# The first stage of a recurrent-mixer layer: the norm's sums from rows of tokens, gates in one bank, two whole tiles in the loop

## The chip, the cores and the metric

The kernel runs on one core of one Trainium2 chip. The metric is the device time of one execution in microseconds (us), the median of several runs; lower is better. A change of about 0.2% is the least that can be told from none.

## The reference, cut to what matters

One layer of a decoder trunk: an RMS norm, one wide input projection, four groups of mixers (mLSTM, Mamba-2 SSD, a gated short convolution, RG-LRU), an output projection with a residual, and a last RMS norm, for 1024 prompt tokens and 8 x 4 sample tokens, 1056 in all, with 2048 channels. The change touches the first lines only:

```python
def rms_norm(x, w):
    x32 = x.astype(jnp.float32)
    y = x32 * lax.rsqrt(jnp.mean(x32 * x32, axis=-1, keepdims=True) + EPS)
    return (y * w.astype(jnp.float32)).astype(x.dtype)
...
xn = rms_norm(x, norm_w)
proj = xn @ w_in
(ml_q, ml_k, ml_v, ml_o, ml_z, ml_i, ml_f, ssd_z, ssd_xbc, ssd_dt,
 sc_b, sc_c, sc_h, sc_z, rg_x, rg_z) = split_columns(proj)
```

ml_o and ml_z are split into 128-column tiles, of which o 0 and z 0 are the first two that the kernel computes; the 16 columns of ml_i, ml_f and ssd_dt are the gates.

## The kernel before, in words

Everything lies with channels on the partitions. The input x arrives as 16 tiles k of 128 channels x 1056 tokens (528.5 KB each with the column of the norm's weights). For fp32 accuracy each operand of a matrix product is cut into a high and a low part: `xsplit` makes xh (ScalarE, L469) and xl = x w - xh (VectorE, L472) of a tile, `w_split` makes wh (ScalarE, L260) and wl (VectorE, L261) of a weight piece of two k by 128 columns (128 KB), and `mm6` multiplies with three products for each k: wh xh (L279), wh xl (L280), wl xh (L281). The norm's factor rstd is not needed for the products: it multiplies their results.

`startup` is the first stage. Its loop goes over ke = 0..7, two k at a time, and computes output tile o 0 whole (three PSUM banks of 352 tokens) and two of the three chunks of z 0 (the chunks are 352 tokens wide): 30 products of 128 x 352 in each pass. PSUM has eight banks: five hold these chunks, three hold the gates (`bg`), whose products (L521, plain fp32, 16 columns of weights) come every second pass, four k for each of three chunks, each k to a partition group of its own. Beside the products, `xsquare` gathers the squares for the norm: the square on ScalarE for even k (L478, L483) and on VectorE for odd k (L481), the sum over k on GpSimd (L484), the last two on VectorE. After the loop the third chunk of z 0 is computed by itself with the weights of tile z 0 loaded and cut a second time (48 products), and only then the ordinary loop over tiles begins (`in_proj`, tile 2 of 56). Beside that third chunk the generator `norm_gates` runs: sums over the partitions by TensorE (L338), the root, rstd on all partitions, then the gates' rows.

What sets the order: each engine runs its own instructions in program order. Work of the mixers is written as generators in two lanes; `tick()`, called after each group of six products in `in_proj`, lets each lane go one step. The queue SP issues loads in program order: a load whose buffer isn't free yet holds up all that stand behind it. The input's tiles have 8 buffers (NS, `stage`); the weights' pieces have 3 raw buffers, 5 more in the first stage, and 4 pairs of cut ones (`whl`): `w_next()` cuts the pieces two ahead of the one in use, and so waits for TensorE to release a pair. `in_proj` takes the four banks of `pj()` in turn, and its tile 2 begins with the bank that held the first chunk of o 0, so it waits until that chunk has been copied out (L538).

## Time and profile before

| | |
|---|---|
| device time, median of 3 runs (lowest, highest) | 1838.86 us (1837.83, 1840.14) |
| profiled execution, first to last instruction (its span) | 1837.4 us |
| TensorE busy / ScalarE / VectorE / GpSimd | 1796.7 / 522.8 / 956.9 / 220.1 us |
| first product of the first stage to the first of tile 2 | 5.04 to 87.48 us |

The profile is of one execution; its time is its span, and no other time of that execution is given. The span leaves out what lies before the first and behind the last instruction; the median of the runs is 1.5 us longer. An engine's busy time is summed over the whole span, so a stage in which it waits must be looked at by itself.

### The profile page before, as it was taken

To read this page: it belongs to the slowest core of one execution; us is meant where nothing else is said; L and a number is where in the kernel's file an instruction comes from. 1 tells how busy PE (TensorE), PEld (TensorE's weight loads), DVE (VectorE), ACT (ScalarE), POOL (GpSimd) and SP (SyncE) were. 2 spreads that over 40 slices of the span, in tenths; PEclk is the share of its full clock that TensorE was granted. 3 is DMA by queue.
4 is the path that set the end of the run, shared out by engine and by line. 5 is a ranking of instruction groups with operands and counts; after the bars stand their busy time and mean duration, and the time that the engine had idled before them with its cause. 6 is when DMAs were issued, how large, how long until landed. Compare 5 with 4: busy or idle time off the path is not lost.

```text
span 1837.4 us, 30141 instructions
## 1 busy us (share of the span) xinstructions
PE 1796.7 (98%) x11443; PEld 1762.0 (96%) x11443; DVE 956.9 (52%) x2026; ACT 522.8 (28%) x1244; POOL 220.1 (12%) x248
## 2 busy tenths in 40 slices
PE   7899999999999999999999999999999999999997
PEld 6799999999999999999999999899999999999997
DVE  8875445434624534655357646643773643333664
ACT  4422222212212211221144213211441432222553
POOL 4200101001002000320000003100000221110121
PEclk8999999999999999999999999999999999999998
DMA  6211222212222111331211124321111643332674
GB/s 209 85 47 50 70 58 76 63 60 73 54 70 71 58 59 47 107 77 56 88 43 61 55 69 100 71 82 56 59 58 47 220 125 93 93 93 89 208 251 142
DMA packets 141230, 160.57 MB, mean 87 GB/s; under 512 B 18917, under 2 KB 127997, under 8 KB 140573
## 3 DMA queue, kind: packets, MB, share of 16 engines
q1 hardware_dynamic: 135644, 138.34, 25.4%
q0 software_dynamic: 4704, 18.84, 2.6%
q8 instruction: 89, 1.46, 0.3%
q10 hardware_dynamic: 736, 1.48, 0.3%
q14 instruction: 57, 0.46, 0.1%
HBM read 136.75 MB, written 21.84 MB: 86 GB/s over the span
## 4 chain that ended last, share of the span: by engine, by line
PE 83%; DMA 4%; DVE 3%; issue 1%; ACT 1%; POOL 1%; SPq 0%; DVEq 0%; POOLq 0%; ACTq 0%
PE bank L279 27%; PE bank L281 26%; PE bank L280 26%; DMA arena<-rowd 2%; DVE wl L261 1%; DMA wr<-in_w_in 1%; POOL arena L1073 1%; DVE arena L1082 0%; PE bank L897 0%; PE bank L875 0%; PE bank L896 0%; ACT wh L260 0%; PE bank L899 0%; ACT arena L1060 0%; DMA wr<-in_w_out 0%
## 5 line engine op out<-in xcount | busy, mean ns | idle before, releaser
L279 PE MATMUL bank<-xh,wh 128*128 128x352 f32 x3328 | 1088.3, 327 | 3.2 <-ACT xh L469 2.2
L280 PE MATMUL bank<-xl,wh 128*128 128x352 f32 x3328 | 1076.6, 323 | 13.6 <-DVE xl L472 13.6
L281 PE MATMUL bank<-xh,wl 128*128 128x352 f32 x3328 | 1075.6, 323 | 5.9 <-DVE wl L261 5.7
L280 PEld LDWEIGHTS bank<-xl,wh 128*128 128x128 f32 x3328 | 628.6, 189 | 18.3 <-DVE xl L472 17.9
L279 PEld LDWEIGHTS bank<-xh,wh 128*128 128x128 f32 x3328 | 628.3, 189 | 14.1 <-issue 6.8
L281 PEld LDWEIGHTS bank<-xh,wl 128*128 128x128 f32 x3328 | 628.9, 189 | 7.6 <-DVE wl L261 7.6
L261 DVE TENSOR_TENSOR wl<-wr,wh 128x256 fp32r<-128x256 f32 x540 | 246.1, 466 | 402.7 <-ACT wh L260 401.8
L260 ACT ACTIVATE wh<-wr 128x256 fp32r<-128x256 f32 x540 | 215.6, 412 | 583.7 <-PE bank L280 482.1
L590 DVE TENSOR_TENSOR arena<-bank,arena 128x352 f32<-128x352 f32 x114 | 58.7, 523 | 80.8 <-PE bank L281 80.5
L261 DVE TENSOR_TENSOR wl<-arena,wh 128x256 fp32r<-128x256 f32 x108 | 63.9, 611 | 63.8 <-ACT wh L260 63.3
L1359 POOL TENSOR_TENSOR arena<-arena 128x352 f32<-128x352 f32 x39 | 37.0, 950 | 245.0 <-ACT arena L1358 244.6
L260 ACT ACTIVATE wh<-arena 128x256 fp32r<-128x256 f32 x108 | 42.4, 411 | 78.4 <-PE bank L280 75.0
L941 DVE SCALAR_TENSOR_TENSOR arena<-arena 128x1080 f32<-128x1080 f32 (+1 forms) x44 | 59.9, 1361 | 1.0
L1351 DVE TENSOR_TENSOR arena<-bank,arena 128x352 f32<-128x352 f32 x47 | 24.7, 525 | 41.8 <-PE bank L281 20.1
L1358 ACT ACTIVATE arena<-arena 128x352 f32<-128x352 f32 x44 | 22.0, 500 | 79.9 <-DVE arena L1351 79.9
L279 PE MATMUL bank<-xh,xl 128*128 128x352 f32 x128 | 41.5, 324 | 0.0
L281 PE MATMUL bank<-xh,xl 128*128 128x352 f32 x128 | 41.4, 324 | 0.0
L280 PE MATMUL bank<-xl 128*128 128x352 f32 x128 | 41.1, 321 | 0.0
L929 POOL COPY arena<-arena 128x3 f32<-128x3 f32 (+1 forms) x16 | 3.0, 186 | 296.1 <-DVE arena L585 296.1
L583 DVE TENSOR_TENSOR arena<-bank,arena 128x352 f32<-128x352 f32 x32 | 16.4, 522 | 41.5 <-PE bank L281 41.5
L484 POOL TENSOR_TENSOR arena<-arena 128x1056 f32<-128x1056 f32 x13 | 32.6, 2510 | 35.6 <-DVE arena L481 35.1
L405 DVE RECIPROCAL arena<-arena 128x352 f32<-128x352 f32 (+3 forms) x18 | 35.7, 1981 | 0.2
(332 smaller groups left out, 1288.1 us busy)
## 6 DMA issues: line engine op xcount, KB each, us to landing
wr<-in_w_in SPq DMA_DIRECT2D x441, 128.0 KB, 2.4
wr<-in_w_out SPq DMA_DIRECT2D x130, 128.0 KB, 2.7
arena<-in_w_out SPq DMA_DIRECT2D x126, 128.0 KB, 2.6
arena<-rowd SPq DMA_DIRECT2D x32, 256.0 KB, 5.1
arena<-in_x SPq DMA_DIRECT2D x15, 528.5 KB, 6.3
mixd<-arena POOLq DMA_DIRECT2D x15, 528.0 KB, 3.9
arena<-mixd SPq DMA_DIRECT2D x15, 528.0 KB, 5.9
arena<-in_x SPq DMA_DIRECT2D x16, 352.0 KB, 3.4
```

Source lines behind the costliest of these rows:

```text
L260: self.S.activation(h, r, AF.Copy)
L261: self.V.tensor_sub(l, r, h.bitcast(F32))
L279: self.P.matmul(bank[:, :n], wh[:, k, :], xh, start=first and k == 0, stop=False)
L280: self.P.matmul(bank[:, :n], wh[:, k, :], xl, start=False, stop=False)
L281: self.P.matmul(bank[:, :n], wl[:, k, :], xh, start=False, stop=last and k == 1)
L405: self.V.reciprocal(x[:, a:b], x[:, a:b])
L484: (V if k > 13 else G).tensor_add(acc[:, :NT], acc[:, :NT], sq[k % 2][:, :NT])
L590: V.tensor_mul(a[:, t0:t0 + CH], bank[:, :CH], rs[:, t0:t0 + CH])
L941: V.scalar_tensor_tensor(y[:, :n], a[:, i:i + n], w(i), y[:, :n], op0=OP.mult, op1=OP.add)
L1351: V.tensor_add(y[:, ts], b[:, :w], y[:, ts])
L1358: S.activation(t, y[:, ts], AF.Square)
L1359: (G if nacc[gr] < KT - 1 else V).tensor_add(a[:, ts], a[:, ts], t)
```

## The change

- x is loaded a second time, from a copy in DRAM with tokens as rows (`xr`, 1056 x 2048), in 18 pieces of 128 tokens x 1024 channels (512 KB; the last two have 32 tokens). For each, `rsum` is one ScalarE instruction: the square with its sum along the row into a column of `sums`. `xsquare`, its buffers, GpSimd's adds, VectorE's squares and the sum over partitions by TensorE are gone; `col_rsqrt` adds two columns of `sums` instead.
- The gates lie in one bank: for each k four products of 264 tokens, each token quarter to a partition group of its own, directly behind the products of that pass. Two banks become free.
- z 0 is computed whole in the loop (36 products in each pass); the third chunk's loop and the second load of its weights are gone.
- x has 6 buffers instead of 8, the rows 5. x tile k+6 is loaded behind the gates of k, and row piece k behind that. x tile 1 comes in thirds. `xsplit` of a pass stands one pass ahead.
- The 14 loads of constants move from SP's queue, pass 3, to GpSimd's queue, pass 1.
- `norm_gates` starts with tile 2 instead of with the third chunk.

```diff
-        for n in range(1, len(TILES)):
+        for n in range(2, len(TILES)):
...
-            if self.wi < 18 or not any(r is a for a in self.spare):
+            if self.wi < 10 or not any(r is a for a in self.spare):
...
-    def col_rsqrt(self, acc, w, mul, add, dst, drop=False):
...
+    def col_rsqrt(self, sums, w, mul, add, dst):
...
-        bk = self.mx()
-        for c in range(nb):
-            n = min(128, w - 128 * c)
-            P.matmul(bk[:n, c:c + 1], acc[:, 128 * c:128 * c + n], self.ones, start=True, stop=True)
-        if drop:
-            acc.drop()
-        yield 2
-        V.tensor_scalar(v[:, :nb - 1], bk[:, :nb - 1], mul, add, op0=OP.mult, op1=OP.add)
...
-        V.tensor_scalar(v[:m, nb - 1:], bk[:m, nb - 1:nb], mul, add, op0=OP.mult, op1=OP.add)
+        V.tensor_add(v, sums[:, :nb], sums[:, nb:2 * nb])
+        sums.drop()
+        V.tensor_scalar(v, v, mul, add, op0=OP.mult, op1=OP.add)
...
-            Q.dma_start(a[:src.shape[0], :src.shape[1]], src)
+            self.G.dma_start(a[:src.shape[0], :src.shape[1]], src)
...
-        NS = 8
+        NS, NX, GW = 6, 5, NT // 4
         stage = [self.slot() for _ in range(NS - 1)] + [self.rstd]
-        sq = [self.slot() for _ in range(2)]
-        acc = self.slot()
+        rows = [self.slot() for _ in range(NX)]
...
+        nb = (NT + 127) // 128
+        sums = self.take(2 * nb)
+        V.memset(sums.ap, 1.0)
...
-        Q.dma_start(stage[0][:, 0:CH + 1], self.io["x"][:, 0, 0:CH + 1])
-        self.w_load(1)
-        for c in (1, 2):
-            e = slice(CH * c + 1, CH * c + CH + 1)
-            Q.dma_start(stage[0][:, e], self.io["x"][:, 0, e])
-        self.w_load(2)
-        xload(1)
-        self.w_load(3)
-        xload(2)
-        Q.dma_start(wg.ap, self.io["w_g"].rearrange("p k c -> p (k c)"))
-        self.w_load(4)
-        for k in range(3, NS):
-            xload(k)
-            self.w_load(k + 2)
...
+        def xload(k, parts=1, other=None):
+            n = NT // parts
+            for c in range(parts):
+                e = slice(n * c + (c > 0), n * c + n + 1)
+                Q.dma_start(stage[k % NS][:, e], self.io["x"][:, k, e])
+                if c == 0 and other:
+                    other()
+        def rload(i):
+            if i < 2 * nb:
+                b, h = i // 2, i % 2
+                n = min(128, NT - 128 * b)
+                Q.dma_start(rows[i % NX][:n, :D // 2], self.io["xr"][128 * b:128 * b + n, D // 2 * h:D // 2 * h + D // 2])
+        def rsum(i):
+            if i < 2 * nb:
+                b, h = i // 2, i % 2
+                n = min(128, NT - 128 * b)
+                r = rows[i % NX][:n, :D // 2]
+                S.activation(r, r, AF.Square, accum_out=sums[:n, nb * h + b:nb * h + b + 1])
...
-        def xsquare(k):
-            x = stage[k % NS][:, 1:NT + 1]
-            if k == 0:
-                S.activation(acc[:, :NT], x, AF.Square)
-            else:
-                if k % 2:
-                    V.tensor_mul(sq[k % 2][:, :NT], x, x)
-                else:
-                    S.activation(sq[k % 2][:, :NT], x, AF.Square)
-                (V if k > 13 else G).tensor_add(acc[:, :NT], acc[:, :NT], sq[k % 2][:, :NT])
+        xload(0, 3, lambda: self.w_load(1))
+        self.w_load(2)
+        xload(1, 3)
+        Q.dma_start(wg.ap, self.io["w_g"].rearrange("p k c -> p (k c)"))
+        self.w_load(3)
+        for k in range(2, NS):
+            xload(k)
+            self.w_load(k + 2)
...
-        bz = [self.pj(), self.bank[7]]
-        bg = self.bank[4:7]
+        bz = [self.pj(), self.bank[7], self.bank[6]]
+        bg = self.bank[4]
+        def gates(k):
+            for c in range(4):
+                P.matmul(bg[32 * c:32 * c + 16, :GW], wg3[:, k, 0:16], stage[k % NS][:, GW * c + 1:GW * c + GW + 1],
+                         start=k == 0, stop=k == KT - 1)
+            if k + NS < KT:
+                xload(k + NS)
...
                 self.w_split(2)
-                xsplit(1)
-            else:
-                xsplit(2 * ke)
-                xsplit(2 * ke + 1)
-            for k in (2 * ke, 2 * ke + 1):
...
-            if ke == 0:
+                xsplit(1, 3)
                 V.tensor_mul(wg3[:, :, 0:16], wg3[:, :, 0:16], wg3[:, :, 16:17].to_broadcast([128, KT, 16]))
-            if ke == 3:
-                self.const_loads()
-            if ke:
-                for banks in (bo, bz):
-                    wh, wl = self.w_next()
-                    for c, b in enumerate(banks):
-                        self.mm6(b, wh, wl, ke, CH * c, CH, False, ke == 7)
-            else:
                 w2 = [self.w_next(), self.w_next(0)]
+                xsplit(2)
                 for k in range(2):
                     for banks, w in zip((bo, bz), w2):
                         for c, b in enumerate(banks):
                             self.mm6(b, *w, 0, CH * c, CH, True, False, (k,))
-            if ke % 2:
-                for c in range(3):
-                    for k in range(2 * ke - 2, 2 * ke + 2):
-                        j = 32 * (k % 4)
-                        P.matmul(bg[c][j:j + 16, :CH], wg3[:, k, 0:16], stage[k % NS][:, CH * c + 1:CH * c + CH + 1],
-                                 start=ke == 1, stop=ke == 7)
-                for k in range(2 * ke - 2, 2 * ke + 2):
-                    if k + NS < KT:
-                        xload(k + NS)
-        for a in (*sq, *stage[:-1], wg):
+                xsplit(3)
+            else:
+                for i, banks in enumerate((bo, bz)):
+                    if 2 * ke + 2 + i < KT:
+                        xsplit(2 * ke + 2 + i)
+                    wh, wl = self.w_next()
+                    for c, b in enumerate(banks):
+                        self.mm6(b, wh, wl, ke, CH * c, CH, False, ke == 7)
+            if ke == 1:
+                self.const_loads()
+            for i in {2: (0, 1, 2), 3: (3, 4), 4: (5, 6), 5: (7, 8), 6: (9, 10), 7: (11, 12, 13)}.get(ke, ()):
+                rsum(i)
+            for k in (2 * ke, 2 * ke + 1):
+                gates(k)
+                rload(k)
+        rload(16)
+        rload(17)
+        for i in range(14, 2 * nb):
+            rsum(i)
+        for a in (*stage[:-1], wg):
...
-        o, z, g = self.slot(), self.slot(), self.slot()
-        for c in (1, 0):
+        o, z, g = self.slot(), self.slot(), self.take(GW)
+        for c in range(3):
+            S.activation(o[:, CH * c:CH * c + CH], bo[c][:, :CH], AF.Copy)
             V.tensor_copy(z[:, CH * c:CH * c + CH], bz[c][:, :CH])
-        for c in range(3):
-            S.activation(g[:, CH * c:CH * c + CH], bg[c][:, :CH], AF.Copy)
-        self.lanes[0].append(self.norm_gates(acc, g, o, z))
-        for ke in range(8):
-            wh, wl = self.w_next()
-            self.mm6(self.bank[7], wh, wl, ke, 2 * CH, CH, ke == 0, ke == 7)
-            if ke < 3:
-                S.activation(o[:, CH * ke:CH * ke + CH], bo[ke][:, :CH], AF.Copy)
-            self.tick()
-        S.activation(z[:, 2 * CH:NT], self.bank[7][:, :CH], AF.Copy)
+        S.activation(g.ap, bg[:, :GW], AF.Copy)
+        for a in rows:
+            a.drop()
...
+        self.lanes[0].append(self.norm_gates(sums, g, o, z))
...
-        yield 2
-        yield from self.col_rsqrt(acc, NT, 1.0 / D, EPS, self.rstd[:, :NT], True)
+        yield 3
...
-        for c in range(3):
+        n = NT // 4
+        for c in range(4):
             b = self.mx()
-            ts = slice(CH * c, CH * c + CH)
-            P.matmul(b[:72, :CH], self.selg.ap, g[:, ts], start=True, stop=True)
+            ts = slice(n * c, n * c + n)
+            P.matmul(b[:72, :n], self.selg[32 * c:32 * c + 16, :], g[32 * c:32 * c + 16, :], start=True, stop=True)
             yield 1
-            V.tensor_mul(gt[:72, ts], b[:72, :CH], self.rstd[:72, ts])
+            V.tensor_mul(gt[:72, ts], b[:72, :n], self.rstd[:72, ts])
```

(Comments and empty lines are left out; the host adds `a["xr"] = c(x[:, 1:].T)`.)

ScalarE at the end of the loop and behind it; wh is a cut weight piece, arena the working memory, bank_81 to bank_83 are o 0's chunks, bank_85 holds gates. Before:

```order
L469 ACTIVATE xh<-arena 128x1056 x2
L483 ACTIVATE arena<-arena 128x1056
L260 ACTIVATE wh_74<-arena 128x256
L260 ACTIVATE wh_76<-arena 128x256
L469 ACTIVATE xh<-arena 128x1056 x2
L483 ACTIVATE arena<-arena 128x1056
L260 ACTIVATE wh_70<-wr_67 128x256
L260 ACTIVATE wh_72<-wr_68 128x256
L532 ACTIVATE arena<-bank_85 128x352
L532 ACTIVATE arena<-bank_86 128x352
L532 ACTIVATE arena<-bank_87 128x352
L260 ACTIVATE wh_74<-wr_69 128x256
```

The same place now:

```order
L468 ACTIVATE xh<-arena 128x1056
L260 ACTIVATE wh_76<-arena 128x256
L461 ACTIVATE arena<-arena 128x1024 x2
L260 ACTIVATE wh_70<-wr_67 128x256
L260 ACTIVATE wh_72<-wr_68 128x256
L461 ACTIVATE arena<-arena 128x1024 x5
L461 ACTIVATE arena<-arena 32x1024 x2
L533 ACTIVATE arena<-bank_81 128x352
L533 ACTIVATE arena<-bank_82 128x352
L533 ACTIVATE arena<-bank_83 128x352
L535 ACTIVATE arena<-bank_85 128x264
L260 ACTIVATE wh_74<-wr_69 128x256
```

Seven row sums now stand together behind the last two cut weights, and the copies of o 0 that free the banks stand behind them.

TensorE at the end of pass 1 (bank_88 is z 0's second chunk, bank_87 was gates and is now z 0's third chunk):

```order
 L281 MATMUL bank_88<-xh,wl_77 128x352
-L521 MATMUL bank_85<-arena 16x352 x4
-L521 MATMUL bank_86<-arena 16x352 x4
-L521 MATMUL bank_87<-arena 16x352 x4
+L279 MATMUL bank_87<-xh,wh_76 128x352
+L280 MATMUL bank_87<-xl,wh_76 128x352
+L281 MATMUL bank_87<-xh,wl_77 128x352
+L279 MATMUL bank_87<-xh,wh_76 128x352
+L280 MATMUL bank_87<-xl,wh_76 128x352
+L281 MATMUL bank_87<-xh,wl_77 128x352
+L492 MATMUL bank_85<-arena 16x264 x8
```

Six products of the third chunk come into each pass, and the gates come as eight shorter products in every pass instead of twelve in every second one.

SP's queue from pass 2 to pass 3, before (in_x is x, in_w_in weights, in_params the first of the constants):

```order
L249 DMA wr_68<-in_w_in 128x256
L249 DMA wr_69<-in_w_in 128x256
L249 DMA arena<-in_w_in 128x256 x3
L442 DMA arena<-in_x 128x1057 x4
L249 DMA arena<-in_w_in 128x256 x2
L392 DMA arena<-in_params 128x112
```

And now (in_xr are the rows):

```order
L249 DMA arena<-in_w_in 128x256 x2
L446 DMA arena<-in_x 128x1057
L454 DMA arena<-in_xr 128x1024
L446 DMA arena<-in_x 128x1057
L454 DMA arena<-in_xr 128x1024
L249 DMA wr_67<-in_w_in 128x256
```

Each pass now issues two tiles of x and two pieces of rows between its weights, where x came in fours every second pass. Beyond the first few tiles (some 350 us) every engine's instructions stand in the same order in both kernels.

## Rows read from the trace of the kernel before

**Rows 1.** The page's first parts: the span, and TensorE's granted clock by fortieths of it.

```profile
span 1837.4 us, 30141 instructions
...
PEclk8999999999999999999999999999999999999998
```

**Rows 2.** Busy us by engine in long stretches, granted clock, DMA share, GB/s.

```profile
core 0: us, PE busy (x) PEld busy (x) DVE busy (x) ACT busy (x) POOL busy (x), PEclk, DMA share, GB/s
0.00:88.00 88.00, 70.88 (x418) 60.01 (x419) 74.19 (x74) 39.78 (x60) 32.83 (x17) 0.90 0.44 149
88.00:200.00 112.00, 111.84 (x705) 110.20 (x704) 67.06 (x119) 28.88 (x63) 2.75 (x4) 1.00 0.17 50
```

**Rows 3.** The same view by 5 us, of the first stage.

```profile
5.00:10.00 5.00, 3.37 (x16) 2.68 (x15) 1.54 (x4) 2.17 (x4) 0.00 (x0) 1.00 0.96 301
10.00:15.00 5.00, 3.49 (x15) 3.25 (x16) 4.43 (x4) 4.86 (x6) 1.79 (x1) 0.82 1.03 405
15.00:20.00 5.00, 1.25 (x5) 0.80 (x4) 5.00 (x3) 4.32 (x7) 3.20 (x2) 0.50 0.81 312
20.00:25.00 5.00, 5.00 (x22) 4.57 (x21) 5.00 (x5) 0.42 (x1) 2.98 (x2) 0.66 0.09 28
...
30.00:35.00 5.00, 4.41 (x27) 4.12 (x27) 5.00 (x4) 1.30 (x3) 3.83 (x2) 1.00 1.00 386
```

**Rows 4.** Waits up to 88 us: total us, times, longest.

```profile
POOL arena L484 <- DVE arena L481: 35.1, 7, 12.8
...
PE bank L280 <- DVE xl L472: 13.6, 10, 3.7
...
PE bank L279 <- ACT xh L469: 2.2, 1, 2.2
```

**Rows 5.** Groups by shape up to 88 us: busy us, mean ns, idle before.

```profile
L484 POOL TENSOR_TENSOR arena<-arena 128x1056 f32<-128x1056 f32 x13 | 32.6, 2510 | 35.6 <-DVE arena L481 35.1
L472 DVE SCALAR_TENSOR_TENSOR xl<-arena,xh 128x1056 fp32r<-128x1056 f32 x15 | 30.0, 2037 | 3.3 <-ACT xh L469 3.3
...
L261 DVE TENSOR_TENSOR wl<-arena,wh 128x256 fp32r<-128x256 f32 x15 | 19.5, 1327 | 1.9 <-ACT wh L260 1.6 <-PE bank L280 0.2
L469 ACT ACTIVATE xh<-arena 128x1056 fp32r<-128x1056 f32 x15 | 16.9, 1163 | 2.7 <-DMA arena<-in_x 2.6
...
L483 ACT ACTIVATE arena<-arena 128x1056 f32<-128x1056 f32 x7 | 7.5, 1076 | 0.1
L260 ACT ACTIVATE wh<-arena 128x256 fp32r<-128x256 f32 x15 | 6.1, 416 | 18.4 <-PE bank L280 18.3
```

**Rows 6.** The order of time: start us, us, engine line op; single places.

```profile
5.04 0.50 PE L279 MATMUL bank<-xh,wh 128*128 128x352 f32 x1
...
8.05 0.32 PE L281 MATMUL bank<-xh,wl 128*128 128x352 f32 x1
9.36 1.17 ACT L469 ACTIVATE xh<-arena 128x1056 fp32r<-128x1056 f32 x1 [2.59 <-DMA arena<-in_x]
...
11.94 0.43 PE L280 MATMUL bank<-xl,wh 128*128 128x352 f32 x1 [0.93 <-DVE xl L472]
...
27.24 2.54 DVE L472 SCALAR_TENSOR_TENSOR xl<-arena,xh 128x1056 fp32r<-128x1056 f32 x2
...
33.82 4.71 DVE L472 SCALAR_TENSOR_TENSOR xl<-arena,xh 128x1056 fp32r<-128x1056 f32 x2
...
45.37 1.97 PE L521 MATMUL bank<-arena 128*16 128x352 f32 x24
...
47.28 0.43 PE L279 MATMUL bank<-xh,wh 128*128 128x352 f32 x1
...
78.57 0.46 ACT L538 ACTIVATE arena<-bank 128x352 f32<-128x352 f32 x1
...
87.48 0.32 PE L279 MATMUL bank<-xh,wh 128*128 128x352 f32 x1
```

**Rows 7.** DMA issues of the whole span: size of each, median us to landing.

```profile
arena<-in_x SPq DMA_DIRECT2D x15, 528.5 KB, 6.3
```

More of the change, by code (lines that the diff above doesn't have):

```diff
@@ L433, in startup @@
         self.weights_list()
-        NS = 8
+        NS, NX, GW = 6, 5, NT // 4
         stage = [self.slot() for _ in range(NS - 1)] + [self.rstd]
-        sq = [self.slot() for _ in range(2)]
-        acc = self.slot()
+        rows = [self.slot() for _ in range(NX)]
         wg = self.take(272)
         wg3 = wg.ap.rearrange("p (k c) -> p k c", k=KT)
-        def xload(k):
-            Q.dma_start(stage[k % NS][:, :NT + 1], self.io["x"][:, k, :])
+        nb = (NT + 127) // 128
+        sums = self.take(2 * nb)
+        V.memset(sums.ap, 1.0)
         spare = [self.take(256) for _ in range(3)]
@@ L489, in startup @@
         bo = [self.pj() for _ in range(3)]
-        bz = [self.pj(), self.bank[7]]
-        bg = self.bank[4:7]
+        bz = [self.pj(), self.bank[7], self.bank[6]]
[6 more added lines that the diff above has]
+                xload(k + NS)
+        late_rows = 0
         for ke in range(8):
@@ L543, in startup, with norm_gates @@
             a.drop()
-    def norm_gates(self, acc, g, o, z):
+        self.lanes[0].append(self.norm_gates(sums, g, o, z))
+    def norm_gates(self, sums, g, o, z):
         V, P = self.V, self.P
-        yield 2
-        yield from self.col_rsqrt(acc, NT, 1.0 / D, EPS, self.rstd[:, :NT], True)
+        yield 3
+        yield from self.col_rsqrt(sums, NT, 1.0 / D, EPS, self.rstd[:, :NT])
         self.param_prep()
@@ L1488, in layout @@
     a["x"] = c(x.reshape(KT, 128, NT + 1).transpose(1, 0, 2))
+    a["xr"] = c(x[:, 1:].T)
     w = f("w_in")[0]
```

4 lines of the change are left out of this document (removed).

## The prediction

> **What bounds the kernel now.** I read the page's span and clock first, then busy time in long stretches, then the first stage in steps of 5 us, then who waits for whom there, and last single places in the order of time. The span is 1837.4 us, and the granted clock is at full speed but for the first and the last fortieth [rows 1]. From 88 to 200 us TensorE is busy 111.84 of 112 us; in the first 88 us it is busy 70.88, and its clock is 0.90 of full speed [rows 2]. So nearly all that can be won near the change lies in the first 88 us.
>
> There the steps of 5 us show VectorE busy 5.00 of 5.00 in steps in which TensorE waits: from 15 to 20 us TensorE has 1.25 us of work [rows 3]. The waits name the same engine: 13.6 us for xl (VectorE, L472), 2.2 us for xh [rows 4]. VectorE has not that much to do. Its split of one tile takes 1.27 us where GpSimd is idle (2.54 for two, from 27.24), but the pair from 33.82, beside GpSimd's adds, takes 4.71; over the stage the mean is 2.04 us, and a cut weight piece means 1.33 [rows 5, 6]. GpSimd's 13 adds of 2.51 us are thus paid on VectorE as well. A second loss is the clock: it is 0.82, 0.50 and 0.66 in the steps from 10 to 25 us, which begin when TensorE has waited twice for x tile 1 [rows 3, 6]. The first stage ends, with z 0's third chunk, when tile 2 begins at 87.48 us [rows 6].
>
> **The change, term by term.** I build the new time at which tile 2 begins.
>
> *Start.* The first product stands at 5.04 us [rows 6]; the loads ahead of it are the same. 5.0.
>
> *Products.* 6 chunks x 6 x 8 passes = 288 products, against 240 + 48 before: the same work. Steady pace: 111.84 us for 705 = 0.159 us [rows 2]. 288 x 0.159 = 45.8.
>
> *Slow beginning.* The first 15 products took 5.04 to 8.05 + 0.16 = 3.2 us, 15 x 0.159 = 2.4: 0.8 lost, kept.
>
> *x tile 1.* It landed whole at 9.36; its third chunk's xl was first used at 11.94 or later [rows 6]. In thirds, the last third lands no later than about 9.4, since the bytes ahead of it are the same; split in thirds (1.16 / 3 on ScalarE, 1.27 / 3 on VectorE, with overhead some 0.6 each) its xl stands at 10.6. TensorE wants it after 24 products, at 5.0 + 0.8 + 24 x 0.159 = 9.6. Wait 1.0, between 0 (earlier thirds hide it) and 2.2 (the wait now, [rows 4]).
>
> *Gates.* A group of 12 products (4224 columns) took 45.37 to 47.28 = 1.91 us [rows 6]. A pass now has 8 x 264 = 2112 columns. In proportion to columns: 0.96 x 8 = 7.6; at the pace per instruction (24 records in 1.91 us = 0.080; now 16 records a pass) 1.27 x 8 = 10.2. Both kernels stream four partition groups side by side, so I take columns, and 0.1 for each entry: 8.4, up to 10.9. The Trainium skill (TensorEngine Tiling, Key Properties) says that a change of the tiling mode drains TensorE, and this change doubles the entries, 4 to 8. No row prices the drain by itself; the 1.91 us above holds one.
>
> *VectorE.* A pass has two splits and two cut weights: 2 x 1.27 + 2 x 1.33 = 5.2 us at most, even at the weights' disturbed mean. TensorE's pass is 36 x 0.159 + 1.05 = 6.8. No squares, no GpSimd adds beside it. Cover 1.6 us a pass: 0 on the path, after pass 1; there x tile 4's split stands ahead of the second weight piece, 0.5 us.
>
> *ScalarE.* A pass has two splits of 1.16, two cut weights of 0.42 and 2 to 3 row sums. The trace has no sum along a row; its square alone took 1.08 on 1056 columns [rows 5], so 1.04 on 1024, and at most 0.42 more (a whole small instruction, the cut of a weight). I take 1.1: 5.6 to 6.5 us, against 6.8. It hides; without cover a pass would grow by the difference.
>
> *Row loads.* By the end of the loop x 8.7 MB, rows 8.7, some 24 weight pieces 3.1, gates' weights and constants 0.7 land: 21.2 MB. Steps with loads queued moved 386 and 405 GB/s, the first 301 [rows 3]: 52 to 55 us at the high rates, from about 3 us on. So loads end at 55 to 58 us, before the loop's end. x itself has six buffers: tile k+6 is asked for three passes (20 us) ahead of its use, and lands in 6.3 us [rows 7]. 0 on the path, if the rate holds.
>
> *End of the loop.* ScalarE cuts the last weights when TensorE has ended pass 6, about 7 us before the loop's end; seven row sums (7.7 us) stand behind, and the three copies of o 0 (0.46 each, [rows 6]) behind these. Tile 2 waits for the first copy: 7.7 + 0.4 + 0.5 - 6.8 - 0.8 = 1.0 us, between 0 and 4 (sums at 1.46). Before, tile 2 had no such wait.
>
> *Constants, norm.* Constants go past SP's queue onto an idle GpSimd; nothing needs them before the transposes, some 9 us into tile 2. `norm_gates` starts eight ticks later against the tiles; rstd must stand before tile 2's results are taken out at its 22nd tick, and its chain has 13. 0. TensorE's sums over partitions (inside the 87.48) are gone, the gates' rows cost the same columns.
>
> Sum: 5.0 + 45.8 + 0.8 + 1.0 + 8.4 + 0.5 + 1.0 = 62.5 us against 87.48: 25.0 us less. The rest of the program stands in the same order and TensorE is full there, so the gain stays. Span 1837.4 - 25.0 = 1812.4; the median of the runs is 1.5 above the span: **1813.9 us**, 1.4% faster.
>
> **Rivals.** (1) *The clock falls again.* Before, it stood below full speed from 10 to 25 us [rows 3], after two waits. If the wait for x tile 1 is enough again, and TensorE works through 10 us at 0.5 to 0.66, some 4 us are lost: 1818. For it: the same start. Against: one short wait in place of two longer ones, and the wait for xl at 15 us is gone.
>
> (2) *Rows come late, or row sums are dear.* At 301 GB/s [rows 3] 21.2 MB take 70 us, and the last rows would hold up the copies of o 0 by some 10 us, since tile 2 waits for them: 1824; at 350 GB/s by 3 us: 1817. Against: 386 and 405 in loaded steps. The Trainium skill (HBM Reference, Specifications) gives a core 358 GB/s, but also says that a core alone gets more; an estimate by 358 alone has the loads end near 62 us and the time at about 1816. The trace's 405 does not bear the lower figure out here.
>
> (3) *Something else bounds the stage*, so that only VectorE's extra goes and a new stall takes half: 1826. For it: the stage has five engines and one queue within 20% of each other. Against: each has its own slack above.
>
> (4) *Slower.* SP's order and ScalarE's order now form a ring: row piece 4 is issued behind x tile 10, both behind the gates of k = 4 at the end of pass 2, and ScalarE must take that row's sum before it may split x tile 10, which pass 5 needs. Two passes, 13.6 us, must hold the landing and 1.1 + 1.16 + 1.27 us: landings up to 10 us cost nothing, each us above that half a us in each pass. Passes 2 to 7 stand in the ring, from about 20 us on. To lose they must take (87.5 - 20) / 6 = 11.2 us each, so landings over 19 us, where the median now is 6.3 [rows 7]. At 25 us they take 14.2 each, tile 2 begins at 106, and the kernel takes 1858.
>
> **How the numbers follow.** The forecast's case, 1811 to 1817 by the bounds of gates, wait and sums, has 0.65; rival 1 0.12 (1815 to 1819), rival 2 0.13 (1816 to 1824), rival 3 0.06, rival 4 0.02, and 0.02 that it is the same for a reason I don't see. The range 1810 to 1821 leaves out rivals 3 and 4 and the end of 2. About 0.2% is what a measurement of this kernel tells from no change: faster 0.95, same 0.02, slower 0.03.
>
> **What would show it.** Right: tile 2's first product at 61 to 64 us; TensorE without waits for xl from 20 us on; splits at 1.27 us each; a granted clock of 1.0 from 10 us; GpSimd idle but for its DMA issues; a wait of about 1 us for ScalarE at tile 2's start; the later program unmoved but for the offset. Wrong: TensorE waiting on ScalarE or x in the passes; gates over 1.3 us a pass; a row sum well over 1.1 us; landings of x over 10 us; a step at half clock after 10 us; new waits between 62 and 200 us.

## The result and the profile after

The changed kernel takes 1825.22 us (median of 4 runs, 1822.03 to 1826.11), beside 1839.5 for the kernel before on the same chip: a ratio of 0.9922, 95% interval 0.9908 to 0.9936, 14 us faster. Predicted were 1813.9, 25 us faster, and a range of 1810 to 1821. The direction was right, the size was not. The profiled execution has a span of 1824.3 us, 13.1 below that of [rows 1].

The changed kernel's trace in the long stretches of [rows 2], and in four of its first 75 us: busy time of each engine, granted clock, DMA share, GB/s.

```profile
0.00:88.00 88.00, 80.08 (x534) 69.97 (x535) 36.91 (x72) 51.61 (x90) 7.85 (x18) 0.98 0.71 245
...
88.00:200.00 112.00, 112.00 (x706) 110.63 (x705) 69.13 (x123) 27.15 (x59) 2.59 (x4) 1.00 0.18 50
...
5.00:55.00 50.00, 47.66 (x341) 40.93 (x340) 25.82 (x35) 33.95 (x55) 3.92 (x8) 1.00 1.01 361
...
60.00:65.00 5.00, 4.55 (x39) 3.60 (x37) 1.58 (x3) 1.15 (x2) 0.00 (x0) 1.00 0.69 225
65.00:70.00 5.00, 1.26 (x7) 1.26 (x8) 0.01 (x1) 4.88 (x12) 0.00 (x0) 0.96 0.00 0
70.00:75.00 5.00, 5.00 (x24) 5.00 (x23) 3.36 (x17) 0.68 (x2) 0.00 (x0) 0.70 0.19 52
```

VectorE is busy 36.91 us of the first 88 instead of 74.19, and TensorE 80.08 instead of 70.88. The largest hole is from 65 to 70 us, where TensorE works 1.26 of 5 us, and behind it the granted clock is 0.70: for part of the step TensorE runs at 1.2 instead of 2.4 GHz. From 5 to 55 us the DMA engines are full (share 1.01) and move 361 GB/s.

The changed kernel's groups by shape up to 88 us, as [rows 5]: busy us, mean ns, idle before.

```profile
L471 DVE SCALAR_TENSOR_TENSOR xl<-arena,xh 128x1056 fp32r<-128x1056 f32 x14 | 18.4, 1316 | 22.5 <-ACT xh L468 22.5
L461 ACT ACTIVATE arena<-arena 128x1024 f32<-128x1024 f32 x16 | 16.8, 1052 | 11.4 <-DMA arena<-in_xr 11.4
...
L261 DVE TENSOR_TENSOR wl<-arena,wh 128x256 fp32r<-128x256 f32 x10 | 4.1, 419 | 0.0
...
L461 ACT ACTIVATION_READ_ACCUMULATOR arena<-arena 128x1 f32 x16 | 3.0, 186 | 0.0
```

A split takes 1316 ns instead of 2037, a cut weight 419 instead of 1327. The new row sum is 1052 ns and a second record of 186 ns; VectorE now idles for ScalarE, and ScalarE's sums for rows.

The order of time around the end of the loop, ScalarE's rows and then TensorE's (start us, us), as [rows 6]:

```profile
58.84 1.05 ACT L461 ACTIVATE arena<-arena 128x1024 f32<-128x1024 f32 x1
...
62.60 1.06 ACT L461 ACTIVATE arena<-arena 128x1024 f32<-128x1024 f32 x1 [2.62 <-DMA arena<-in_xr]
...
65.12 1.06 ACT L461 ACTIVATE arena<-arena 128x1024 f32<-128x1024 f32 x1 [1.37 <-DMA arena<-in_xr]
...
67.21 1.04 ACT L461 ACTIVATE arena<-arena 32x1024 f32<-32x1024 f32 x1
...
68.25 1.13 ACT L533 ACTIVATE arena<-bank 128x352 f32<-128x352 f32 x3
...
57.51 0.43 PE L279 MATMUL bank<-xh,wh 128*128 128x352 f32 x1
...
63.45 1.09 PE L492 MATMUL bank<-arena 128*16 128x264 f32 x16
68.74 0.43 PE L279 MATMUL bank<-xh,wh 128*128 128x352 f32 x1 [4.20 <-ACT arena L533]
```

The loop ends with the gates at 64.5 us. Tile 2 waits 4.2 us for the copies of o 0 at 68.25; they stand in ScalarE's order behind the last four row sums, and two of those waited for their rows, until 62.60 and 65.12. The reason for that lies in the queue of loads:

```profile
56.77 0.89 SPq L249 DMA_DIRECT2D wr<-in_w_in  x2
57.72 1.84 SPq L454 DMA_DIRECT2D arena<-in_xr  x4
```

The last four row pieces are issued only from 57.72 us on, behind loads of weights, which wait for ScalarE and VectorE to cut what lies in their buffers; the buffer of the first of the four was free when its last sum ended, at 54.85 us. This is read from the order in the queue; no run has these loads in another order. Tile 2 begins at 68.74 instead of 87.48: 18.7 us are won there, 13.1 are left at the end of the span.

### The profile page after: what moved, and what is told of

The parts are those of the page before. It is cut to its first block, busy times and chain, and to the rows that moved or that the text cites. A ratio compares the mean times of both kernels' runs of the same rounds, so it can differ in the third digit from the quotient of the medians.

```text
span 1824.3 us, 30163 instructions
## 1 busy us (share of the span) xinstructions
PE 1792.2 (98%) x11459; PEld 1758.1 (96%) x11459; DVE 915.5 (50%) x2012; ACT 529.4 (29%) x1263; POOL 195.4 (11%) x249
## 4 chain that ended last, share of the span: by engine, by line
PE 91%; DMA 3%; DVE 2%; ACT 1%; issue 1%; SPq 1%; POOL 0%; DVEq 0%; ACTq 0%; POOLq 0%
PE bank L279 29%; PE bank L281 29%; PE bank L280 28%; DMA arena<-rowd 1%; DMA wr<-in_w_in 1%; DVE wl L261 1%; DVE arena L1081 0%; PE bank L896 0%; PE bank L874 0%; PE bank L895 0%; DMA arena<-in_x 0%; POOL arena L1072 0%; PE bank L1110 0%; DMA arena<-in_xr 0%; PE bank L898 0%
## 5 line engine op out<-in xcount | busy, mean ns | idle before, releaser
L261 DVE TENSOR_TENSOR wl<-wr,wh 128x256 fp32r<-128x256 f32 x537 | 239.5, 456 | 400.8 <-ACT wh L260 400.1
L261 DVE TENSOR_TENSOR wl<-arena,wh 128x256 fp32r<-128x256 f32 x103 | 48.3, 487 | 62.4 <-ACT wh L260 62.4
L471 DVE SCALAR_TENSOR_TENSOR xl<-arena,xh 128x1056 fp32r<-128x1056 f32 (+1 forms) x20 | 21.7, 1096 | 24.0 <-ACT xh L468 24.0
```

What stands on the lines that cost most here:

```text
L261: self.V.tensor_sub(l, r, h.bitcast(F32))
L471: V.scalar_tensor_tensor(self.xl[:, k, ts], x, w, self.xh[:, k, ts].bitcast(F32), op0=OP.mult, op1=OP.subtract)
```

## Experiments

All times are medians; ratios are to the kernel before on the same chip.

### The changed kernel and three edits of its last row sums, its constants and its rows

**Unchanged**, for the comparison. 

> The changed kernel once more, nothing altered. In its profile tile 2 began at 68.7 us, 18.7 us earlier than before, but the span was only 13.1 us shorter: about 2.6 us went to half clock right behind the wait at the loop's end, 3.3 us in two stages at some 787 and 1154 us. Theory A (the later loss is luck of where DMA waits fall): this run's later loss differs by a microsecond or more and may be near 0. Rival B (it follows from the change): again about 3 us at the same two places.

Measured: 1826.21 us, 0.992 (0.9908 to 0.9933). Tile 2 begins at 69.61 after a wait of 3.26 us. Of the 17.9 us won there 13.3 are left at the end of the span, so 4.6 us are lost later instead of 5.6. A low clock near 790 us comes again, one near 1154 us does not, so each theory holds in part. The loop ends 1.8 us later than in the first profile, and the clock from 15 to 20 us makes some 1.7 of it (0.34 x 5 us), first profile and this one:

```profile
15.00:20.00 5.00, 4.07 (x24) 3.83 (x25) 4.52 (x6) 3.23 (x5) 0.00 (x0) 1.00 1.05 376
```

```profile
15.00:20.00 5.00, 3.89 (x13) 3.65 (x14) 4.61 (x6) 3.36 (x6) 0.00 (x0) 0.66 1.06 382
```

TensorE's waits for xh and xl from 5 to 30 us are 2.3 us in the first and 2.1 us in this one. What decides between the two clocks is not shown.

**Copies first.** 

```diff
-        for i in range(14, 2 * nb):
-            rsum(i)
         for a in (*stage[:-1], wg):
...
             V.tensor_copy(z[:, CH * c:CH * c + CH], bz[c][:, :CH])
+        for i in range(14, 2 * nb):
+            rsum(i)
```

> The three copies of o 0 stand ahead of the last four row sums on ScalarE; all else as in the change. Theory A (the late rows cost time only because the copies stand behind their sums): the wait of 4.2 us ahead of tile 2 goes, and with it the stretch at half clock behind it; tile 2 begins at about 64.6, and the time falls by 4.2 + 2.6 = 6.8 us to 1818.5. Rival B (tile 2 waits for something else soon after, the norm's factor, which now ends as late as before against a tile that started earlier): the wait moves into tile 2 or 3 and the time stays within 2 us of 1825.

Measured: 1820.13 us, 0.9887 (0.9874 to 0.9901), 6.1 us below the unchanged one. Its stretches at the same place:

```profile
60.00:65.00 5.00, 5.00 (x40) 4.48 (x42) 1.58 (x3) 3.17 (x7) 0.00 (x0) 1.00 0.84 254
65.00:70.00 5.00, 5.00 (x37) 4.65 (x30) 0.58 (x2) 4.42 (x10) 0.00 (x0) 1.00 0.02 7
70.00:75.00 5.00, 5.00 (x33) 5.00 (x32) 3.15 (x17) 0.42 (x1) 0.00 (x0) 1.00 0.28 82
```

The wait is gone, and so is the low clock behind it. ScalarE's sums take as long as before, but nothing waits for them. The mechanism is theory A's; the time fell by 6.1 us, not 6.8.

**Five rows only.** The loads of row pieces 5 to 17 are left out; their sums run on what lies in the buffers.

```diff
         def rload(i):
-            if i < 2 * nb:
+            if i < NX:
```

> Only the first five pieces of the rows are loaded (2.6 of 8.7 MB); all 18 row sums run, on what the five buffers hold, so the norm's sums are not the reference's. Theory A (DMA is full from 5 to 55 us and the last rows land late; the sums themselves fit): the waits of the sums for rows go, tile 2 waits less than 1 us and starts at about 64 us; with no half clock the time is 1817 to 1819. Rival B (ScalarE's own work of seven sums at 1.13 us holds the copies up): the wait stays over 3 us.

Measured: 1820.26 us, 0.9887 (0.9872 to 0.9902). All 18 sums still run ahead of the copies, and TensorE has no wait for them (5.00 of 5.00 us from 60 to 70 us). So it is the rows' late landing that holds the copies, not the work of the sums. The loop ends some 2 us later than in the first profile, as in the second: the granted clock is 0.67 from 15 to 20 us here.

**Constants held.** The loads on GpSimd's queue are put behind a one-column copy that needs x tile 8's xl.

```diff
-            if ke == 1:
+            if ke == 3:
+                G.tensor_copy(self.gtmp[:, 0:1], self.xl[:, 8, 0:1].bitcast(F32))
                 self.const_loads()
```

> One small GpSimd copy that reads xl of tile 8 stands ahead of the 14 loads of constants, so that they start in pass 3 (some 31 us) instead of at 1.3 us. Theory A (the constants on GpSimd's queue, which nothing holds back, take DMA time from x tiles 2 and 3): x tile 3 lands 1 to 1.5 us earlier than 13.7, the waits of 0.5 and 0.9 us in pass 1 go, and the loop ends 1.5 to 2 us earlier, at about 62.8; the rows still come late, so tile 2 gains less than that, 0 to 2 us: 1823 to 1825. Rival B (x tiles 2 and 3 are late because of the weights and gates' weights queued between them): x tile 3 lands at 13.7 as before and nothing moves.

Measured: 1824.51 us, 0.9912 (0.9899 to 0.9926). The loop's last gates begin at 64.27 us, between the 63.45 and 65.26 of the unchanged kernel's two profiles, and tile 2 at 69.87 after a wait of 4.50: where the loop ends sooner, the wait is longer. The granted clock from 15 to 20 us is 0.66 here, as in the second of the two profiles, and beside that one the loop ends 1.0 us sooner. By its median the edit can't be told from none.

**Both.** 

> The changed kernel with the copies of o 0 and z 0 ahead of the last four row sums and with the constants held back to pass 3. Theory A, that the two losses are separate (the wait at tile 2's start about 6 us, the early bytes of the constants 1 to 1.7 us): 1818 to 1819.5 us, a tile 2 that starts without a wait for ScalarE at 64 to 64.8 us. Rival B, that the constants only move the queue of loads, so that what pass 1 gains is lost at another landing: 1820 to 1821.5, as with the copies alone.

Measured: 1817.23 us, 0.9884 (0.987 to 0.9897); once more, on another chip:

> The version with copies first and constants held, once more, for a second profile and for the comparison with the two runs beside it. It gained 23.4 us against before's profile by 500 us of the program and had 21.9 of them at its end. Theory A, that the loss near 800 us belongs to this program: 0.8 to 2.5 us are lost there again, and about 1.4 at the end. Rival B, that it varies: under 0.5 us there. Time 1816 to 1819.5.

Measured: 1819.25 us, 0.9889 (0.9873 to 0.9906). Tile 2 begins at 63.94 and 64.06 us without a wait, with the copies alone at 65.36. In these three the granted clock is 1.00 from 10 to 25 us. Among the profiles with that clock the loop ends 0.4 to 1.4 us sooner with the constants held (last gates at 62.91 and 63.04, beside 63.45, 63.94 and 64.33 in the unchanged kernel, with the wait filled and with the copies alone). The ratios can't be told apart, so the medians do not show what the early constants cost.

**The wait filled.**

```diff
+        for i in range(24):
+            P.matmul(self.bank[5][:, :CH], self.xl[:, KT - 1, 0:128], self.xl[:, KT - 1, 0:CH], start=True, stop=True)
         self.lanes[0].append(self.norm_gates(sums, g, o, z))
```

> The changed kernel with 24 more products of 128 x 352, whose result nobody reads, between the loop and tile 2, so that TensorE works through the 4.2 us in which it now waits for ScalarE's copy of o 0. They take 24 x 0.16 = 3.8 us. Theory A, that the half clock of 69.8 to 73.2 us follows from the wait: tile 2 begins within 0.7 us of 68.7, no half clock follows it, and the time falls by 1.5 to 3 us against the changed kernel, to 1822 to 1824. Rival B, that the clock falls there whatever TensorE did before: half clock behind tile 2's start as now, time 1825 to 1827. Rival C, that the fill delays tile 2 by its own length: 1828 to 1830.

Measured: 1824.4 us, 0.9925 (0.9912 to 0.9939). The fill in the order of time, and the stretch behind it:

```profile
64.96 4.13 PE L542 MATMUL bank<-xl 128*128 128x352 f32 x24
```

```profile
70.00:75.00 5.00, 5.00 (x33) 5.00 (x32) 3.33 (x17) 1.14 (x4) 0.00 (x0) 1.00 0.26 74
```

Tile 2 begins at 69.20, and the clock stays at 1.00 (2.4 GHz) from 70 to 75 us where it was 0.70. So the low clock follows the wait. In the profile it costs some 1.5 us: up to the row of the next table at 735 us the unchanged kernel keeps 16.9 of the 18.7 us won at tile 2, this one 18.0 of 18.3. The median of its runs doesn't show a gain, and theory A's 1822 to 1824 us was missed by 0.4.

### The kernel before and the adds on GpSimd

**No adds.** GpSimd's thirteen adds are left out, so the norm's sum is incomplete.

```diff
-                (V if k > 13 else G).tensor_add(acc[:, :NT], acc[:, :NT], sq[k % 2][:, :NT])
+                if k > 13:
+                    V.tensor_add(acc[:, :NT], acc[:, :NT], sq[k % 2][:, :NT])
```

> The kernel before, with GpSimd's thirteen adds of squares left out (the norm's sum is then not the reference's). Theory A, that these adds slow VectorE's splits: the split of one x tile falls from the 2.04 us of the profile before to 1.27 to 1.32 us with VectorE's own work otherwise unchanged, the products' wait for xl falls from 13.6 us to under 4, and tile 2 begins 8 to 14 us earlier than 87.48 us; time 1825 to 1831 us. Rival B, that VectorE's own squares and cut weights bound the stage: splits at 1.3 us, but a wait for xl of 8 us or more and tile 2 less than 5 us earlier; time over 1834. Rival C, that the adds cost VectorE nothing: splits stay near 2 us.

Measured: 1818.31 us, 0.9889 (0.9875 to 0.9902), 20.5 us faster than the kernel with them and faster than the changed kernel. Tile 2 begins at 67.19 us, 20.3 earlier: theory A's mechanism, with more than the 8 to 14 us that it gave. Its groups by shape, its first 88 us, and what is left of the waits for xl:

```profile
L472 DVE SCALAR_TENSOR_TENSOR xl<-arena,xh 128x1056 fp32r<-128x1056 f32 x15 | 19.2, 1317 | 4.7 <-ACT xh L469 4.7
...
L261 DVE TENSOR_TENSOR wl<-arena,wh 128x256 fp32r<-128x256 f32 x15 | 6.0, 423 | 3.6 <-ACT wh L260 3.5
```

```profile
0.00:88.00 88.00, 83.34 (x541) 74.39 (x542) 56.53 (x97) 46.60 (x75) 0.20 (x4) 1.00 0.47 158
```

```profile
PE bank L280 <- DVE xl L472: 1.8, 3, 0.9
```

A split takes 1317 ns and a cut weight 423, as in the changed kernel, although nothing else was changed. VectorE still has its squares (56.53 us busy). The clock is 1.00. The adds made 11.8 of the 13.6 us of waits for xl [rows 4] and nearly all of what the clock lost, 0.90 [rows 2]; the next run shows that a part of the low clock can stay without them.

**The adds moved.** All squares on ScalarE, all adds on VectorE; the whole computation is done.

```diff
-                if k % 2:
-                    V.tensor_mul(sq[k % 2][:, :NT], x, x)
-                else:
-                    S.activation(sq[k % 2][:, :NT], x, AF.Square)
-                (V if k > 13 else G).tensor_add(acc[:, :NT], acc[:, :NT], sq[k % 2][:, :NT])
+                S.activation(sq[k % 2][:, :NT], x, AF.Square)
+                V.tensor_add(acc[:, :NT], acc[:, :NT], sq[k % 2][:, :NT])
```

> The kernel before, whole, with GpSimd taken out of the norm: all squares on ScalarE, all adds of them on VectorE. Theory A, that the adds cost what they did because they ran on GpSimd beside VectorE: by the shapes of the run without adds, VectorE has in the loop 15 splits of 1.32, 16 cut weights of 0.42 and 15 adds of 1.26 us, some 47 us, and ScalarE some 43, of the 60 that TensorE needs; tile 2 begins at 66 to 70 us and the time is 1817 to 1822 us. Rival B, that the adds cost by being work in the chain, wherever they run: waits for xl of 5 us or more, tile 2 later than 74 us, 1826 us or more.

Measured: 1820.86 us, 0.9902 (0.9887 to 0.9917), as theory A had it; tile 2 begins at 69.3 us. By the medians these few lines gain more than the change did, though the intervals overlap (the change: 0.9908 to 0.9936). The clock, which was 1.00 without the adds, falls once here with GpSimd just as idle:

```profile
15.00:20.00 5.00, 4.20 (x15) 3.91 (x16) 4.90 (x8) 5.00 (x8) 0.00 (x0) 0.66 0.88 329
```

### The changed loop without row loads

Squares on ScalarE, adds on VectorE or on GpSimd, the sum over partitions by TensorE as before; copies first and constants held in both.

```diff
-            for i in {2: (0, 1, 2), 3: (3, 4), 4: (5, 6), 5: (7, 8), 6: (9, 10), 7: (11, 12, 13)}.get(ke, ()):
-                rsum(i)
+            for k in (2 * ke, 2 * ke + 1):
+                xsquare(k)
```

> The changed loop (copies first, constants held) without the row loads: squares of x on ScalarE, their adds on VectorE, and the sum over partitions on TensorE as in the kernel before. Theory A, that the second load of x costs about what it saves: loads no longer fill the DMA engines, the first passes lose 1 to 2 us less, tile 2 begins at 62.3 to 63.3 us, and the sum over partitions takes about 2 us of TensorE after that; 1815.5 to 1818. Rival B, that the squares and adds bound the loop: VectorE has 2 x 1.32 + 2 x 0.42 + 2 x 1.26 = 6.0 us in a pass of 6.98 and ScalarE 5.3; if that is too tight, passes of 7.4 us or more and 1821 or more.

Measured: 1823.6 us, 0.9916 (0.9902 to 0.9929), beside 1817.2 and 1819.25 with rows. Tile 2 begins at 64.62 (with rows 63.94), so the passes did not bind, and the missing loads don't help. Of the difference, 2.0 us are the sum over partitions, in the order of time:

```profile
68.56 1.99 PE L338 MATMUL bank<-arena 128*128 128x1 f32 x18
```

The rest is lost later; it is in the table below. Theory A's time missed, and rival B's time came without its mechanism: the passes take 7.0 us, not 7.4.

> The same as the loop without rows, but with the adds on GpSimd, as in the kernel before. Theory A, that what GpSimd's adds cost is the time in which VectorE's splits stand still, and that it comes to the end of the program only where VectorE has no slack: splits beside an add take 2.0 to 2.5 us again, VectorE has about 6.0 us in a pass of 6.98, passes stay within 0.4 us, time within 3 us of the loop with the adds on VectorE. Rival B, that any add on GpSimd beside the splits comes back in full, about 1.5 us each: passes of 9 us or more, 1832 us or more.

Measured: 1836.28 us, 0.9984 (0.9976 to 0.9993): with the adds on GpSimd the changed loop is nearly as slow as the kernel before. Theory A fell, and rival B's time came. GpSimd's row and VectorE's in the order of time:

```profile
19.89 11.97 POOL L464 TENSOR_TENSOR arena<-arena 128x1056 f32<-128x1056 f32 x4 [1.65 <-ACT arena L463]
...
19.96 3.53 DVE L474 SCALAR_TENSOR_TENSOR xl<-arena,xh 128x1056 fp32r<-128x1056 f32 x1
23.41 2.69 DVE L261 TENSOR_TENSOR wl<-arena,wh 128x256 fp32r<-128x256 f32 x1
26.02 3.53 DVE L474 SCALAR_TENSOR_TENSOR xl<-arena,xh 128x1056 fp32r<-128x1056 f32 x1
29.48 2.67 DVE L261 TENSOR_TENSOR wl<-arena,wh 128x256 fp32r<-128x256 f32 x1
32.07 1.30 DVE L474 SCALAR_TENSOR_TENSOR xl<-arena,xh 128x1056 fp32r<-128x1056 f32 x1
33.30 0.41 DVE L261 TENSOR_TENSOR wl<-arena,wh 128x256 fp32r<-128x256 f32 x1
```

Beside adds of 3.0 us each (11.97 / 4) a cut weight of 0.42 us takes 2.7 and a split of 1.32 takes 3.5: each record is some 2.2 us longer. The last two rows stand behind the adds, which end at 31.86 us, and take 1.30 and 0.41 again. The mean add is 2.83 us, so a pass has 2 x 2.83 + 2 x 1.32 + 2 x 0.42 = 9.1 us if nothing of it overlaps, against 6.98 of TensorE; its passes 2 to 7, from 23.52 to 79.82 us, take 9.4 on the mean. Single passes take 7.0 to 13.2 us, since GpSimd adds nothing from 31.86 to 43.96 us, where the held constants stand in its order, and then 29.00 us without a break; the clock is also low in the last two of them, 0.69 from 60 to 65 us and 0.50 from 70 to 75. So the mean agrees with the sum, but it does not test it pass by pass. My 6.0 us counted an add at VectorE's 1.26, which left a slack that isn't there. The Trainium skill (SBUF — State Buffer, two separate sides) says that of a GpSimd instruction that reads SBUF and a VectorE instruction with two inputs there, the one that starts first has their shared port pair for its whole length, and the other blocks. The rows agree: splits and cut weights have two such inputs, and grow only beside adds.

### Gates in pairs, thirds of more x tiles

Both on the version with copies first and constants held.

```diff
-            for k in (2 * ke, 2 * ke + 1):
+            for k in range(2 * ke - 2, 2 * ke + 2) if ke % 2 else ():
                 gates(k)
+            for k in (2 * ke, 2 * ke + 1):
                 rload(k)
```

> The version with copies first and constants held, and the gates' products of two passes together in every second pass, so that TensorE enters them four times instead of eight. A pass now takes 6.98 us where 36 x 0.159 + 1.06 give 6.78. Theory A, that these 0.2 us and about 0.1 us more in the group itself come at each entry: two passes together take 13.6 to 13.7 us instead of 13.96, the loop ends 1.0 to 1.4 us earlier, time 1815.8 to 1816.3. Rival B, that an entry costs nothing: 13.9 to 14.0 and 1817.2. Rival C, that x tiles, released a pass later, come late: waits for xh in the odd passes, 1818 or more.

Measured: 1823.11 us, 0.9913 (0.9899 to 0.9926), 4 to 6 us slower. Rival C: x tiles are asked for a pass later, and ScalarE's splits wait for them (waits up to 90 us: total, times, longest):

```profile
ACT xh L468 <- DMA arena<-in_x: 22.4, 10, 9.7
```

Its gates of the second pair, in the order of time:

```profile
23.47 1.99 PE L492 MATMUL bank<-arena 128*16 128x264 f32 x32
25.39 0.43 PE L279 MATMUL bank<-xh,wh 128*128 128x352 f32 x1
```

The gates of four k take 25.39 - 23.47 = 1.92 us, those of two 63.94 - 62.91 = 1.03 in the version that it was made from: an entry costs about 0.1 us in the group, far less than the landings.

```diff
-            xload(k)
+            xload(k, 3 if k < 4 else 1)
...
-                xsplit(2)
+                xsplit(2, 3)
...
-                xsplit(3)
+                xsplit(3, 3)
```

> The version with copies first and constants held, with x tiles 2 and 3 also loaded and split in thirds. In its profile TensorE waits 1.6 us for xl from 10 to 20 us, behind splits that wait for the whole tile to land. Theory A, that the wait for whole tiles is the cause: waits for xl under 0.6 us there, tile 2 begins 0.8 to 1.5 us earlier, 1815.7 to 1816.5. Rival B, that the bytes come no sooner and six splits of a third cost more than two whole ones: no gain, 1817 to 1818.5.

Measured: 1818.96 us, 0.989 (0.9875 to 0.9904), beside 1819.25 for the version without. The waits for xl are gone from 5 to 26 us, 1.2 us for a cut weight take their place, and tile 2 begins at 63.63 instead of 64.06. No gain that can be told.

### Where the later microseconds go

> The kernel before, unchanged, for a second profile. The changed kernel's three profiles lose 1.2 to 2.4 us against the first profile of before near 790 us and 0.5 to 1.6 us at the end, in code that the change does not touch. Theory A, that this belongs to where the change shifts the loads of the stage: the second profile of before is like its first there, without half clock from 780 to 800 us. Rival B, that it varies from run to run: the second profile of before shows a wait of 2 us or more for VectorE and some 3 us at half clock there too.

Measured: 1836.45 us, one run. Near 790 us it is like the first profile, without a low clock, as theory A had it, but its end comes 1.8 us sooner against its middle.

> The whole kernel before with GpSimd out of the norm (1820.9 us), and the norm's generator, with all mixers' work behind it, eight ticks later against the tiles, as the change has it. Theory A, that the change's later losses come from this shift: 1.5 to 3 us slower, 1822.4 to 1824, with a loss near 800 us or at the end that the version without the delay does not show. Rival B, that the shift costs nothing (from about 380 us on the instructions of VectorE and ScalarE stand in the same order in both kernels): 1820 to 1821.8, and no loss there.

Edit of the second one, on the kernel before with the adds moved: `yield 2` becomes `yield 10` at the head of `norm_gates`. Measured: 1819.81 us, 0.9893 (0.9878 to 0.9908); the one without the delay had 0.9902. One instruction of the SSD mixer stands at two places of the program; its first and last start tell how far each kernel is ahead there. Its row (shortest, median and longest in ns, first and last start in us) in the kernel before, the changed one, and the version with both edits:

```profile
L1017 DVE TENSOR_TENSOR arena<-arena x2: 418/420/422, 751.7 to 1102.7; 128x256 f32<-128x256 f32 x2
```

```profile
L1016 DVE TENSOR_TENSOR arena<-arena x2: 416/417/418, 734.8 to 1087.1; 128x256 f32<-128x256 f32 x2
```

```profile
L1017 DVE TENSOR_TENSOR arena<-arena x2: 420/420/420, 728.3 to 1080.3; 128x256 f32<-128x256 f32 x2
```

The same differences for the other profiles, in us ahead of the first profile of before:

| | at 752 | at 1103 | end of span |
|---|---|---|---|
| changed kernel | 16.9 | 15.6 | 13.1 |
| the same once more | 16.1 | 13.7 | 13.3 |
| copies first | 22.0 | 20.0 | 20.4 |
| both edits, two profiles | 23.4, 23.2 | 22.4, 20.7 | 22.1, 19.1 |
| changed loop without rows | 20.7 | 17.7 | 15.7 |
| before, second profile | 0.5 | 0.9 | 2.7 |
| before without adds | 20.2 | 20.6 | 21.1 |
| before, adds moved | 18.4 | 17.5 | 18.4 |
| the same, lanes later | 19.9 | 18.7 | 18.1 |

Between the two places the kernels with the changed loop lose 0.8 to 3.0 us (the six profiles that are not in the table: 0.8 to 2.3), those with the loop of before -0.4 to 1.2. A part of this is the clock. From 790 to 795 us in the kernel before, the changed one, and the changed one once more:

```profile
790.00:795.00 5.00, 5.00 (x39) 4.68 (x38) 3.61 (x7) 1.43 (x6) 1.90 (x2) 1.00 0.29 67
```

```profile
790.00:795.00 5.00, 5.00 (x30) 4.45 (x29) 4.09 (x11) 2.57 (x8) 0.62 (x1) 0.67 0.10 28
```

```profile
790.00:795.00 5.00, 4.04 (x19) 3.40 (x20) 4.18 (x10) 2.85 (x10) 1.47 (x2) 0.66 0.09 26
```

Such a step, some 1.7 us lost, stands between 785 and 815 us in seven of the twelve profiles with the changed loop and in none of the five with the loop of before. The seven lose 1.3 to 3.0 us between the two places, the other five 0.8 to 1.6. Behind it the profiles scatter by 2 us in both directions, the kernel before among them. The delay of the lanes makes no difference that the medians show. Why the clock falls there in some executions of the changed loop, and why the others still lose some 1 us, stays open.

## Why the prediction missed, step by step

**Right: what bounded the stage.** GpSimd's adds were paid on VectorE, and taking them away ends the waits for xl: splits of 1316 ns, cut weights of 419. The mechanism is shown from both sides, by the kernel before without the adds (20.5 us faster) and by the changed loop with them (nearly all lost again). The prediction gave the start's waits for x a share of the low clock as well. That is neither shown nor excluded: without the adds, and with those waits, the clock is 1.00 throughout, and with the adds on VectorE it is 0.66 from 15 to 20 us.

**Products, start, gates, VectorE.** The first two passes were to end at 5.0 + 0.8 + 1.0 + 72 x 0.159 + 2 x 1.05 + 0.5 = 20.9 us and end at 22.60, 1.7 later. The first pass ends at 13.15, 0.4 sooner than its part of the sum: in thirds, x tile 1 was waited for no more, where 1.0 stood. The second takes 9.45 us instead of 7.3, because TensorE waits for x tile 3, whose landing the prediction left out there:

```profile
13.68 1.18 ACT L468 ACTIVATE xh<-arena 128x1056 fp32r<-128x1056 f32 x1 [1.31 <-DMA arena<-in_x]
...
16.26 0.43 PE L280 MATMUL bank<-xl,wh 128*128 128x352 f32 x1 [0.93 <-DVE xl L471]
```

The constants, which nothing holds back on GpSimd's queue, load from 1.28 us on and not in pass 1; profiles of the same clock put their cost at 0.4 to 1.4 us. Passes 2 to 7 were to take 6.8 us each and take 7.0: 1.2 us in all. The gates' 0.96 to 1.27 us per pass held.

**Wrong: the row loads, and with them the end of the loop.** The failed step is "Row loads": 21.2 MB at 386 to 405 GB/s, done "at 55 to 58 us, before the loop's end". The rate was 361 GB/s with the DMA engines full for 50 us; the two fast steps of [rows 3] did not stand for it. The Trainium skill (HBM Reference, Specifications) gives a core 358 GB/s, which I had set aside and which the 361 are near. Its remark there that a core streaming alone measures well above this does not fit the mean of these 50 us. But bytes over rate was the wrong reckoning in any case: by the order in the queue the end was set by when the last rows could be issued, 57.72 us, behind weight loads that wait for a buffer. So the term "end of the loop", 1.0 (0 to 4), became 4.2: its working took the seven sums' rows as landed. This is rival 2 at the place that it named: at 350 GB/s it was priced at 3 us, and 3.2 came, in part by luck, since the price was reckoned from bytes and rate alone.

**Wrong: no price for the clock behind that wait.** Rival 1 looked for it behind x tile 1 alone. In the changed kernel's first profile the clock is 1.00 from 10 to 25 us; in its second it is 0.66 from 15 to 20 us, and the loop ends 1.8 us later, so rival 1 came in one execution of the two, at less than half of its 4 us. The wait of 4.2 us is followed by a granted clock of 0.70 from 70 to 75 us, some 1.5 us. With the copies ahead of the sums, wait and low clock go together: 6.1 us, over half of the 11 that were missing.

**Open: "the rest of the program stands in the same order, so the gain stays".** The later program was not unmoved: 0.8 to 3.0 us are lost between 752 and 1103 us by every kernel with the changed loop, in part by a low clock near 790 us; the delay of the lanes was tried and is not shown to be the cause.

**Summed up.** 62.5 became 68.7 by 1.7 (first passes), 1.2 (six passes) and 3.2 (end). Of the 18.7 us then won, 13.1 are left in the profiled span, 14.3 by the medians; of the 5.6 lost, 1.8 go by 735 us, mostly at the low clock behind the wait, 1.3 by 1087 us and 2.5 behind that, where the two profiles of the kernel before differ by 1.8 themselves.

**What the change is worth.** Moving the adds alone gives 0.9902; the change 0.9922; the change with its copies first and its constants held 0.9884 and 0.9889. These last are not told apart from the copies alone (0.9887), from more thirds (0.989), or from the adds moved with the lanes later (0.9893). Rebuilding the loop was not what won most of the time: what it gains beyond moving the adds is 0.2% by the medians at best, and not clear of noise.

## What to carry to other kernels

When an instruction's record is long only beside another engine's work, take that other work away alone, before anything is rebuilt: here thirteen instructions held more than the whole gain. For loads, ask when the queue can issue the last one, not only how long the bytes take. And look at what stands in an engine's order ahead of the copy that frees a bank: work that nobody waits for belongs behind it. Before two profiles are compared by a microsecond or two, compare their granted clocks: one step at the lower level moved the loop's end by 1.8 us in one and the same kernel.

## What the runs showed of the hardware that was not expected

A VectorE instruction of 0.42 us takes 2.7 beside back-to-back adds on GpSimd, so short instructions pay the most, by ratio: 1767 ns mean for ten cut weights in the changed loop with adds on GpSimd. A row sum on 32 partitions takes as long as on 128 (1040 and 1052 ns). Reading its accumulator adds a record of 0.186 us, but consecutive sums start 1.04 us apart (56.76, 57.80, 58.84), so it adds nothing to their pace there.
